# Eight places for the probability rows of attention, and smaller places for output weights and pooled copies

## The chip, the cores and the metric

The kernel runs on one core of a Trainium2 chip. The core has five engines with queues of their own: TensorE (PE in the profile) multiplies matrices out of SBUF into PSUM, VectorE (DVE) and ScalarE (ACT) do elementwise work and read PSUM, GpSimd (POOL) does elementwise work in SBUF alone, and SyncE (SP) issues most of the transfers. Each engine takes its instructions strictly in the order in which the program lists them for it; where an instruction needs what another engine makes, or a place that another engine still reads, it waits, and everything behind it in that queue waits too. The metric is the time of one execution in device microseconds, as the median of several executions.

## The reference

The reference is one layer of a transformer over 1024 latent tokens and 256 context tokens, with 1024 channels, in float32. Two attention branches read the same modulated input. Branch A is windowed (blocks of 128 queries against their neighbours within 128 positions, and the context), branch B is global (every query against all 1280 keys). Each has 8 heads of 64 channels in 2 groups, and rotary positions. Their outputs are multiplied by output weights, gated, added, projected, normalised, and sent through a gated feed-forward network with a short convolution. What this case touches is the middle of it:

```python
def _global_attention(q, k_all, v_all):
    ...
        p = jax.nn.softmax(_gqa_scores(q_blk, k_all), axis=-1)
        return _gqa_values(p, v_all)
...
def _merge_branches(o_a, o_b, gate_logits, w_branch_a, w_branch_b, w_out):
    g_a, g_b = jnp.split(jax.nn.sigmoid(gate_logits), 2, axis=-1)
    return (g_a * (o_a @ w_branch_a) + g_b * (o_b @ w_branch_b)) @ w_out
...
    h = x * (1.0 + scale1) + shift1
    y = _latent_token_mixer(h, kv_ctx, w_in[l], b_in[l], attn_sink[l], q_norm_g[l], k_norm_g[l],
                            w_branch_a[l], w_branch_b[l], w_out[l], rope)
    x = _layer_norm(DEEPNORM_ALPHA * x + gate1 * y, ln1_g[l], ln1_b[l])
    h = x * (1.0 + scale2) + shift2
    y = _conv_ffn(h, w_up[l], conv_w[l], conv_b[l], w_down[l])
    x = _layer_norm(DEEPNORM_ALPHA * x + gate2 * y, ln2_g[l], ln2_b[l])
```

## The kernel before

**Numbers.** TensorE multiplies float32 values that are rounded to a shorter form (`R32`). So each operand is split into a high part `hi`, a rounded copy, and a low part `lo`, the value less `hi`. The helper `split` does both (lines 82 and 84 for `hi`, line 87 for `lo`), on the engines named in its call. A product of two split operands takes three matmuls (`mm3`, lines 90 to 92): high by high, high by low, low by high.

**Stages.** The projections come first (to about 330 us of the span), then attention (to about 766 us), then the rest of the output weights, the output projection, the feed-forward network and the last normalisation.

**Attention units.** The work of attention is cut into 32 units of 128 queries and one group of four heads: units 0 to 15 for branch A, 16 to 31 for branch B. In its loop the program lists, at step u, the score steps of unit u and the value steps of unit u-1, and mixes them by a fraction of the step that each one is given.

- The score steps of a global unit: `cxp(0)` multiplies the queries of heads 0 and 1 by the context keys (256 columns each) into a PSUM tile `sx`, and DVE writes the scaled result into the last 256 columns of the heads' rows `p` and takes a maximum (line 555). `lat(0)` and `lat(1)` multiply by the 1024 latent keys (lines 494 and 495) into a PSUM tile `s` of two banks, DVE writes the first 1024 columns of `p` (line 542), and ACT takes the exponential of the whole row of 1280 and its sum (line 544). `cxp(2)`, `lat(2)` and `lat(3)` do the same for heads 2 and 3. `p` rows come from `p_tile`, with six places of 128 x 1280 float32. A windowed unit takes two such places, each for a pair of heads.
- The value steps of a unit: for each block n of 128 keys (ten in a global unit, four or five in a windowed one) TensorE transposes that block of all four heads' rows into one PSUM bank `ptr` (line 607). ACT casts it to `pth` (line 616), DVE subtracts to `ptl` (line 617). For one block of a windowed unit and two of a global one (`POOL_LO`), ACT copies the bank to `prw` instead (line 613), and POOL splits it. The value matmuls (lines 628 and 629) of a block come three blocks later, or five for the blocks split on POOL in a global unit, and add up in the PSUM tile `av`. After the last, `out_step` copies `av` to `avs` (ACT, line 634), adds its halves, scales them by the row sums, and splits the result into the tiles `O` (POOL mostly). `prw` and `avs` share the tag "ptr" with two places of 2 KB for each partition.

**PSUM.** Its eight banks are three `pt` tiles (for `ptr`, `sx`, the transposed queries, the sums, and the products below), two `s` tiles of two banks, and `av`.

**Output weights.** `branch_steps` multiplies `O` by the output weights of a branch. The loads `ld` fetch eight 128 x 128 blocks, which are two block columns f of the output (512 KB), into one place `wraw`, and POOL splits them into two places of the tag "whl", one for the high half and one for the low. `grp(f, hf)` then does one block column f for half hf of the tokens: 12 matmuls, and a multiplication by the stored gate on DVE (line 944). For branch A these steps are spread over the units 18 to 24 (first half of the tokens) and 25 to 30 (second half), where they stand between the attention steps. For branch B the first two block columns are listed for the end: the load in unit 31, and the four products after the loop. There `first[1]` is column 0 for the first half of the tokens, and the loop over (3, 2, 4) lists column 1 first half, column 0 second half, column 1 second half. Then follow the other block columns, from line 1078 on.

**Places.** `ht` hands out nineteen named places of 4 KB for each partition (`H0` to `H18`), first in first out; `hput` gives them back. During attention they hold the query projections (`Q`, eight), keys (`KL`, four, and `KC`), values (`VT`, five), and later the gated products `bT`.

**Order.** In the attention loop the order on each engine isn't written by hand. The framework's planner lists each engine's instructions by the program's order and by when, by its own cost model, their inputs and places are ready. In the four products after the loop the order on DVE and ACT is that of the program, and TensorE's is the planner's. From the output projection on, TensorE's order is that of the program.

Of the kernel before, what the change touches and what calls it, by code (L numbers as in the profile page):

```python
# [7 lines left out]
F32 = mybir.dt.float32  # L8
R32 = mybir.dt.float32r
# [4 lines left out]
P = 128  # L14
# [6 lines left out]
NK = T + NC  # L21
# [48 lines left out]
def layer_kernel(  # L70
# [6 lines left out]
    nc = tc.nc  # L77
    PSUM = bass.MemoryType.PSUM

    def split(src, hi, lo, hi_eng, lo_eng):  # L80
        if hi_eng is nc.scalar:
            nc.scalar.copy(hi, src)  # L82
        elif hi_eng is nc.gpsimd:
            nc.gpsimd.tensor_scalar(out=hi, in0=src, scalar1=1.0, scalar2=0.0, op0=ALU.mult, op1=ALU.add)
        else:
            hi_eng.tensor_copy(hi, src)
        lo_eng.tensor_tensor(out=lo, in0=src, in1=hi.bitcast(F32), op=ALU.subtract)  # L87

    def mm3(ps, a, b, start, stop, resumed=False):
        nc.tensor.matmul(ps, a[0], b[0], start=start, stop=False, skip_group_check=resumed)  # L90
        nc.tensor.matmul(ps, a[0], b[1], start=False, stop=False, skip_group_check=resumed)  # L91
        nc.tensor.matmul(ps, a[1], b[0], start=False, stop=stop, skip_group_check=resumed)  # L92
# [39 lines left out]
    def ht(name, shape=(P, T), dt=F32):  # L132
        hslot[name] = pool, tag = hfree.pop(0)
        return pool.tile(list(shape), dt, tag=tag, name=name, bufs=1)

    def hput(*names):
        for n in names:
            hfree.append(hslot.pop(n))
# [146 lines left out]
    for k in range(KT):  # L285
# [9 lines left out]
        h, w = hT[k], w0[k]  # L295
# [120 lines left out]
    KL, KC, VT = [], [], []  # L416
# [47 lines left out]
    class Unit:  # L464
# [133 lines left out]
        def value_steps(self):  # L598
            nm, kt = self.id, self.kt
            vh = self.br * 2 + self.g  # L600
            last = self.id == f"1_{NT - 1}_1"
            parts = {}

            def tr_step(n):
                tr = pt_tile(f"ptr{nm}_{n}")
                for h in range(4):
                    nc.tensor.transpose(tr[:, h * P:(h + 1) * P], self.pslice(h, n), ident)  # L607
                hi = att.tile([P, 512], R32, tag="pth", name=f"pth{nm}_{n}", bufs=4)
                lo = att.tile([P, 512], R32, tag="ptl", name=f"ptl{nm}_{n}", bufs=4)
                pooled = n in POOL_LO[self.br] and not last  # L610
                if pooled:
                    rw = att.tile([P, 512], F32, tag="ptr", name=f"prw{nm}_{n}", bufs=2)
                    nc.scalar.copy(rw, tr)  # L613
                    split(rw, hi, lo, nc.gpsimd, nc.gpsimd)
                else:
                    nc.scalar.copy(hi, tr)  # L616
                    nc.vector.tensor_tensor(out=lo, in0=tr, in1=hi.bitcast(F32), op=ALU.subtract)  # L617
                parts[n] = hi, lo
                return pooled

            def av_step(n):
                first = self.left == len(kt)
                self.left -= 1
                if first:
                    self.av = ps2.tile([P, 512], F32, tag="av", name=f"av{nm}")
                hi, lo = parts.pop(n)
                v = VT[kt[n] // 2][:, kt[n] % 2, vh]
                nc.tensor.matmul(self.av, v, hi, start=first, stop=False)  # L628
                nc.tensor.matmul(self.av, v, lo, start=False, stop=self.left == 0)  # L629

            def out_step():
                av = self.av
                avs = att.tile([P, 512], F32, tag="ptr", name=f"avs{nm}", bufs=2)
                nc.scalar.copy(avs, av)  # L634
                up = att.tile([HD, 512], F32, tag="up", name=f"up{nm}", bufs=1)
                nc.gpsimd.tensor_scalar(out=up, in0=avs[HD:P], scalar1=1.0, scalar2=0.0, op0=ALU.mult, op1=ALU.add)
                ot = att.tile([P, 2, P], F32, tag="ot", name=f"ot{nm}", bufs=1)
                oe = nc.gpsimd if self.br and not last else nc.vector
                for h in range(2):
                    oe.tensor_tensor(out=ot[h * HD:(h + 1) * HD],  # L640
                                     in0=avs[0:HD].rearrange("p (a b q) -> p a b q", b=2, q=P)[:, :, h],
                                     in1=up.rearrange("p (a b q) -> p a b q", b=2, q=P)[:, :, h], op=ALU.add)
                nc.gpsimd.tensor_tensor(out=ot, in0=ot, in1=self.rb, op=ALU.mult)
                hf = self.i // 4
                qs = slice((self.i % 4) * P, (self.i % 4 + 1) * P)
                split(ot, otile(self.br, hf, 0, self.g)[:, :, qs], otile(self.br, hf, 1, self.g)[:, :, qs],
                      nc.gpsimd, nc.gpsimd)

            def step(ns):
                pooled = [tr_step(n) for n in ns]  # L650
                for n, pl in zip(ns, pooled):
                    clk[0] += 1
                    avq.append((self, n, clk[0] + LAG[self.br] + (PLAG[self.br] if pl else 0)))
                    av_issue()

            self.left = len(kt)
            self.av_step, self.out_step = av_step, out_step
            g = 1 + self.br
            steps = [lambda n=n: step(range(n, n + g)) for n in range(0, len(kt), g)]
            steps.insert(3 if self.br else 2 if self.i else len(steps), self.rows)  # L660
            return steps
# [127 lines left out]
    turn = [0]  # L789
# [27 lines left out]
    for n, (gi, k) in enumerate(order):  # L817
# [19 lines left out]
        nm, src, tiles = groups[gi]  # L837
# [3 lines left out]
        w, c = ready.pop((gi, k))  # L841
        for t in tiles:
            if t < NT:
                s = slice(t * P, (t + 1) * P)
                a = hT[k][0][:, s], hT[k][1][:, s]
            else:
                s = slice((t - NT) * P, (t - NT + 1) * P)
                a = c[0][:, s], c[1][:, s]
# [36 lines left out]
    att = tc.alloc_tile_pool(name="att", bufs=1, side="right", reuse_waits="tile")  # L885
    ps2 = tc.alloc_tile_pool(name="ps2", bufs=1, space=PSUM, reuse_waits="tile")

    def pt_tile(name, dt=F32):
        return ps2.tile([P, 512], dt, tag="pt", name=name, bufs=3)
# [5 lines left out]
        return s_tile(name)[:, 0:HALF]  # L895

    def p_tile(name):
        return att.tile([P, NK], F32, tag="p", name=name, bufs=6)

    def small(name, shape):  # L900
        return att.tile(list(shape), F32, tag=name.split("_")[0], name=name,
# [19 lines left out]
    def branch_steps(br, wsrc, halves, wpool, engs, f2s=range(4)):  # L921
        steps = []
        w = {}

        def ld(f2, key):
            r = wpool.tile([P, 8, P], F32, tag="wraw", name=f"rwb{br}_{key}", bufs=1)
            nc.sync.dma_start(r, wsrc[f2])
            h = wpool.tile([P, 8, P], R32, tag="whl", name=f"hwb{br}_{key}", bufs=2)
            l = wpool.tile([P, 8, P], R32, tag="whl", name=f"lwb{br}_{key}", bufs=2)
            split(r, h, l, *engs)  # L930
            w[f2] = h, l

        def grp(f, hf, mk):
            if (br, f) not in bT:
                bT[br, f] = ht(f"bT{br}_{f}")
            b = bT[br, f][:, hf * HALF:(hf + 1) * HALF]
            nc.sync.dma_start(b, sgd[br * KT + f][:, hf * HALF:(hf + 1) * HALF])
            wh, wl = w[f // 2]
            ps = mk(f"b{br}_{f}_{hf}")
            for j in range(4):  # L940
                k = (f % 2) * 4 + j
                a = O[br, hf, 0, j // 2][:, j % 2], O[br, hf, 1, j // 2][:, j % 2]
                mm3(ps, (wh[:, k], wl[:, k]), a, j == 0, j == 3)
            nc.vector.tensor_tensor(out=b, in0=ps, in1=b, op=ALU.mult)

        for f2 in f2s:
            steps.append(lambda f2=f2: ld(f2, f"{f2}_{halves[0]}"))
            for f in (2 * f2, 2 * f2 + 1):
                for hf in halves:
                    mk = s_half if br and f % 2 and hf else pt_tile  # L950
                    steps.append(lambda f=f, hf=hf, mk=mk: grp(f, hf, mk))
        return steps

    def done(br, i, g):
# [8 lines left out]
    for u in range(nu + 1):  # L963
        vs, fs = [], []
# [10 lines left out]
        for hf, (u0, u1) in enumerate(FILL):  # L975
# [3 lines left out]
            if u0 <= u < u1:  # L979
                fs = [fill.pop(0) for e in ends if u - u0 <= e < u - u0 + 1]  # L980
# [13 lines left out]
    av_issue(True)  # L994
    nc.sync.dma_start(cvw, conv)
    nc.sync.dma_start(cvb, convb)
    hput("KC", *[f"VT{t}" for t in range(5)])

    def weight(src, nm, n=8, tag="w", he=None, le=None, rtag="raw"):
        if rtag:  # L1000
# [33 lines left out]
    def big(name):  # L1034
        return ps3.tile([P, T], F32, tag="big", name=name, bufs=3)
# [44 lines left out]
    for f in range(2, KT):  # L1080
        bT[1, f] = ht(f"bT1_{f}")
        nc.sync.dma_start(bT[1, f], sgd[KT + f])
        w = wb[f // 2]
        halves = [(0, 1)] if f < KT - 1 else [(0,), (1,)]
        for hs in halves:
            n = HALF * len(hs)
            b = bT[1, f][:, hs[0] * HALF:hs[0] * HALF + n]
            ps = big(f"b1_{f}") if len(hs) == 2 else sml(f"b1_{f}_{hs[0]}")
            for j in range(4):
                k = (f % 2) * 4 + j  # L1090
                for m, hf in enumerate(hs):
                    a = O[1, hf, 0, j // 2][:, j % 2], O[1, hf, 1, j // 2][:, j % 2]
# [233 lines left out]
    for f in (4, 6):  # L1326
        for si in (1, 2):
# [3 lines left out]
            elif f == 6:  # L1331
                (_, st), (_, dg), (_, ca), *ap = ln1(si)
                n = len(pend) - 4
# [42 lines left out]
    wsrc, wtile, wraw = {}, {}, {}  # L1376
# [333 lines left out]
    w = s.stop - s.start  # L1710
# [45 lines left out]
    r = LN2_S[1]  # L1756
# [12 lines left out]
    r = LN2_S[2]  # L1769
# [148 lines left out]
```

## Time and profile before

| What | us |
|---|---|
| Median of 3 executions | 1575.2 |
| Fastest and slowest of them | 1572.35 and 1575.25 |
| The profiled execution | 1573.05 |
| Its span, first to last instruction | 1570.9 |
| First transposition of a windowed unit | 336 |
| First transposition of a global unit | 470 |
| Last value matmul of attention | 766 |

The mean granted TensorE clock of the profiled execution was 0.996 of full speed. In the profile a name such as "p L542" is the tile that an instruction writes and its line in the kernel. A record of a matmul lasts until its modelled end, which lies after the start of the next one, so that records overlap; the time that a matmul takes from the next one is the distance between their starts. An arrow ("<-") in a timeline names what ended an engine's idle time.

### The profile page before, as it was taken

How to read it: one execution, taken by the hardware profiler on the slowest of the kernel's cores; microseconds unless marked ns; L12 is line 12 of the kernel's file. 1: busy time of each engine (PE TensorE's matmuls, PEld its weight loads, DVE VectorE, ACT ScalarE, POOL GpSimd, SP SyncE). 2: the span in 40 equal slices, each digit the busy share in tenths (PEclk: the TensorE clock that was granted, in tenths of full speed). 3: DMA queues.
4: the chain of work that ended last, by engine and by line, in shares of the span. 5: the costliest groups of instructions: out<-in, count | busy, mean ns of one | idle time of the engine just before them, and what ended most of it. 6: DMA issues, size and time to landing. Idle time of an engine off the chain costs nothing.

```text
span 1570.9 us, 22111 instructions
## 1 busy us (share of the span) xinstructions
PE 1535.7 (98%) x7804; PEld 1278.4 (81%) x7804; DVE 1181.4 (75%) x1794; ACT 787.8 (50%) x1287; POOL 754.3 (48%) x699
## 2 busy tenths in 40 slices
PE   9999999999999999999999999999999999999997
PEld 7888888888887777777788998888888888888887
DVE  6677976548887677767774789888888887657884
ACT  5322223358886566666431574544444444435552
POOL 0356423526665666655333445766677774121121
PEclk9999999999999999999999999999999999999998
DMA  9777662322246665630451223233334446996721
GB/s 370 265 239 239 213 244 86 114 76 63 64 134 145 141 163 126 139 79 27 156 187 42 81 84 116 86 118 108 111 115 111 113 113 188 366 268 211 257 98 54
DMA packets 113103, 232.09 MB, mean 148 GB/s; under 512 B 13056, under 2 KB 27904, under 8 KB 112896
## 3 DMA queue, kind: packets, MB, share of 16 engines
q1 hardware_dynamic: 97760, 201.82, 38.1%
q0 software_dynamic: 10400, 20.19, 8.3%
q10 hardware_dynamic: 4832, 8.68, 1.5%
q8 instruction: 61, 1.00, 0.3%
q14 instruction: 50, 0.41, 0.1%
HBM read 179.45 MB, written 65.86 MB: 156 GB/s over the span
## 4 chain that ended last, share of the span: by engine, by line
PE 88%; DVE 7%; ACT 2%; issue 1%; POOL 1%; DMA 0%; SPq 0%; DVEq 0%; ACTq 0%; POOLq 0%
PE ptr L607 6%; PE p L90 4%; PE p L92 4%; PE p L91 4%; PE g L90 4%; PE g L91 4%; PE g L92 4%; PE b L92 3%; PE b L90 3%; DVE p L542 3%; PE b L91 3%; PE av L628 3%; PE av L629 3%; PE s L494 2%; PE c L90 2%; PE c L91 2%
## 5 line engine op out<-in xcount | busy, mean ns | idle before, releaser
L617 DVE TENSOR_TENSOR ptl<-ptr,pth 128x512 fp32r<-128x512 f32 x190 | 124.7, 684 | 40.1 <-ACT pth L616 38.3
L607 PE MATMUL ptr<-ident,p 128*128 128x128 f32 x944 | 144.6, 278 | 8.8 <-ACT prw L613 6.0
L544 ACT ACTIVATE p<-p,nm 128x1280 f32<-128x1280 f32 (+2 forms) x128 | 139.0, 1088 | 20.5 <-DVE p L542 20.4
L607 PEld LDWEIGHTS ptr<-ident,p 128*128 128x128 f32 x944 | 109.4, 141 | 41.7 <-ACT prw L613 10.9
L87 DVE TENSOR_TENSOR ld<-rd,hd 128x1024 fp32r<-128x1024 f32 x77 | 95.0, 1250 | 49.0 <-ACT hd L82 45.3
L616 ACT CAST pth<-ptr 128x512 fp32r<-128x512 f32 x190 | 105.5, 589 | 49.5 <-PE ptr L607 39.8
L82 ACT CAST hd<-rd 128x1024 fp32r<-128x1024 f32 x77 | 79.5, 1050 | 80.4 <-PE p L92 59.0
L87 POOL TENSOR_TENSOR wlg<-wg,whg 128x512 fp32r<-128x512 f32 x32 | 46.8, 1472 | 123.5 <-ACT whg L82 84.5
L90 PE MATMUL p<-hd 128*128 128x512 f32 x264 | 103.2, 391 | 0.0
L92 PE MATMUL p<-hd,ld 128*128 128x512 f32 x264 | 102.8, 389 | 0.0
L91 PE MATMUL p<-ld,hd 128*128 128x512 f32 x264 | 102.7, 389 | 0.0
L628 PE MATMUL av<-pth,VT 128*128 128x512 f32 x236 | 101.4, 430 | 0.7 <-ACT avs L634 0.4
L90 PE MATMUL g<-hh,whg 128*128 128x512 f32 x256 | 99.9, 390 | 0.0
L629 PE MATMUL av<-ptl,VT 128*128 128x512 f32 x236 | 99.4, 421 | 0.4 <-POOL ptl L87 0.4
L92 PE MATMUL g<-hh,wlg 128*128 128x512 f32 x256 | 99.7, 389 | 0.0
L91 PE MATMUL g<-hl,whg 128*128 128x512 f32 x256 | 99.6, 389 | 0.0
L494 PE MATMUL s<-KL,q 128*128 128x512 f32 (+2 forms) x192 | 79.5, 414 | 9.1 <-DVE p L542 7.9
L542 DVE TENSOR_SCALAR_CACHE_REDUCE p<-s,cvt,nmc 128x1024 f32<-128x1024 f32 x64 | 84.5, 1340 | 0.0
L495 PE MATMUL s<-KL,q 128*128 128x512 f32 (+2 forms) x192 | 73.0, 380 | 0.0
L780 ACT ACTIVATE sg<-g,bgc 128x512 f32<-128x512 f32 x32 | 22.0, 686 | 96.2 <-PE g L92 91.5
L82 ACT CAST wS<-s 128x512 fp32r<-128x512 f32 x76 | 45.3, 620 | 46.4 <-POOL s L1220 45.7
L82 ACT CAST wA<-ru 128x512 fp32r<-128x512 f32 x57 | 35.5, 623 | 64.1 <-PE d L92 35.2
(427 smaller groups left out, 4897.6 us busy)
## 6 DMA issues: line engine op xcount, KB each, us to landing
wml<-in_wmodT_dram SPq DMA_DIRECT2D x48, 512.0 KB
ru<-in_w_up_dram SPq DMA_DIRECT2D x38, 512.0 KB
rd<-td SPq DMA_DIRECT2D x55, 256.0 KB
rd<-sd SPq DMA_DIRECT2D x44, 256.0 KB
rd<-in_w_dn_dram SPq DMA_DIRECT2D x33, 256.0 KB
wm<-in_wmodT_dram SPq DMA_DIRECT2D x16, 512.0 KB
wg<-in_w_g_dram SPq DMA_DIRECT2D x32, 256.0 KB
sgd<-sg ACTq DMA_DIRECT2D x32, 256.0 KB
```

Of the source, the lines that this page charges most:

```text
L82: nc.scalar.copy(hi, src)
L87: lo_eng.tensor_tensor(out=lo, in0=src, in1=hi.bitcast(F32), op=ALU.subtract)
L90: nc.tensor.matmul(ps, a[0], b[0], start=start, stop=False, skip_group_check=resumed)
L91: nc.tensor.matmul(ps, a[0], b[1], start=False, stop=False, skip_group_check=resumed)
L92: nc.tensor.matmul(ps, a[1], b[0], start=False, stop=stop, skip_group_check=resumed)
L494: nc.tensor.matmul(o, self.q[0][:, hs], ks, start=True, stop=False)
L542: nc.vector.tensor_scalar(out=out, in0=o, scalar1=self.qscale(nqs)[:, hs] if self.br else -1.0, scalar2=self.other[:, hs], op0=ALU.mult, o ...
L544: nc.scalar.activation(row, row, AF.Exp, bias=self.nm[:, hs], scale=-1.0, accum_out=self.sm[:, hs])
L607: nc.tensor.transpose(tr[:, h * P:(h + 1) * P], self.pslice(h, n), ident)
L617: nc.vector.tensor_tensor(out=lo, in0=tr, in1=hi.bitcast(F32), op=ALU.subtract)
L628: nc.tensor.matmul(self.av, v, hi, start=first, stop=False)
L629: nc.tensor.matmul(self.av, v, lo, start=False, stop=self.left == 0)
```

## The change

The rows `p` get eight places instead of six. The copies `prw` and `avs` leave the tag "ptr" and take, in turn, one half each of a place of `ht` named "side", which is given back after the loop with those of the context keys and values. The output weights are loaded by one block column (256 KB): the raw data have one place ("wraw"), the high parts two ("whl"), the low parts one of their own ("wlo"). The first two columns are loaded in one step, and each further one after the products of the column two before it. The number of matmuls and the elements that are split and copied stay as they were.

```diff
-                    rw = att.tile([P, 512], F32, tag="ptr", name=f"prw{nm}_{n}", bufs=2)
+                    rw = side_tile()
...
-                avs = att.tile([P, 512], F32, tag="ptr", name=f"avs{nm}", bufs=2)
+                avs = side_tile()
...
     def p_tile(name):
-        return att.tile([P, NK], F32, tag="p", name=name, bufs=6)
+        return att.tile([P, NK], F32, tag="p", name=name, bufs=8)
+
+    side = ht("side", (P, 2, 512))
+    turn = [0]
+
+    def side_tile():
+        turn[0] ^= 1
+        return side[:, turn[0]]
...
-        def ld(f2, key):
-            r = wpool.tile([P, 8, P], F32, tag="wraw", name=f"rwb{br}_{key}", bufs=1)
-            nc.sync.dma_start(r, wsrc[f2])
-            h = wpool.tile([P, 8, P], R32, tag="whl", name=f"hwb{br}_{key}", bufs=2)
-            l = wpool.tile([P, 8, P], R32, tag="whl", name=f"lwb{br}_{key}", bufs=2)
+        def ld(f, key):
+            l = wpool.tile([P, 4, P], R32, tag="wlo", name=f"lwb{br}_{key}", bufs=1)
+            r = wpool.tile([P, 4, P], F32, tag="wraw", name=f"rwb{br}_{key}", bufs=1)
+            nc.sync.dma_start(r, wsrc[f // 2][:, (f % 2) * 4:(f % 2) * 4 + 4])
+            h = wpool.tile([P, 4, P], R32, tag="whl", name=f"hwb{br}_{key}", bufs=2)
             split(r, h, l, *engs)
-            w[f2] = h, l
+            w[f] = h, l
...
-        for f2 in f2s:
-            steps.append(lambda f2=f2: ld(f2, f"{f2}_{halves[0]}"))
-            for f in (2 * f2, 2 * f2 + 1):
-                for hf in halves:
-                    mk = s_half if br and f % 2 and hf else pt_tile
-                    steps.append(lambda f=f, hf=hf, mk=mk: grp(f, hf, mk))
+        fs = [f for f2 in f2s for f in (2 * f2, 2 * f2 + 1)]
+        steps.append(lambda: [ld(f, f"{f}_{halves[0]}") for f in fs[:2]])
+        for n, f in enumerate(fs):
+            for hf in halves:
+                mk = s_half if br and f % 2 and hf else pt_tile
+                steps.append(lambda f=f, hf=hf, mk=mk: grp(f, hf, mk))
+            if n + 2 < len(fs):
+                steps.append(lambda f=fs[n + 2]: ld(f, f"{f}_{halves[0]}"))
...
-    hput("KC", *[f"VT{t}" for t in range(5)])
+    hput("KC", "side", *[f"VT{t}" for t in range(5)])
```

More of the change, by code (lines that the diff above doesn't have):

```diff
@@ L937, in grp @@
             nc.sync.dma_start(b, sgd[br * KT + f][:, hf * HALF:(hf + 1) * HALF])
-            wh, wl = w[f // 2]
+            wh, wl = w[f]
             ps = mk(f"b{br}_{f}_{hf}")
             for j in range(4):
-                k = (f % 2) * 4 + j
                 a = O[br, hf, 0, j // 2][:, j % 2], O[br, hf, 1, j // 2][:, j % 2]
-                mm3(ps, (wh[:, k], wl[:, k]), a, j == 0, j == 3)
+                mm3(ps, (wh[:, j], wl[:, j]), a, j == 0, j == 3)
             nc.vector.tensor_tensor(out=b, in0=ps, in1=b, op=ALU.mult)
-        for f2 in f2s:
-            steps.append(lambda f2=f2: ld(f2, f"{f2}_{halves[0]}"))
-            for f in (2 * f2, 2 * f2 + 1):
-                for hf in halves:
-                    mk = s_half if br and f % 2 and hf else pt_tile
-                    steps.append(lambda f=f, hf=hf, mk=mk: grp(f, hf, mk))
+        fs = [f for f2 in f2s for f in (2 * f2, 2 * f2 + 1)]
[6 more added lines that the diff above has]
+                steps.append(lambda f=fs[n + 2]: ld(f, f"{f}_{halves[0]}"))
         return steps
```

## The prediction

> **What bounds the kernel now.** I read the page first, parts 1 and 2, for what is busy.
>
> ```profile
> span 1570.9 us, 22111 instructions
> PE 1535.7 (98%) x7804; PEld 1278.4 (81%) x7804; DVE 1181.4 (75%) x1794; ACT 787.8 (50%) x1287; POOL 754.3 (48%) x699
> ```
>
> TensorE is busy for 98% and nothing else comes near, so at first sight only 35 us (1570.9 less 1535.7) are to be had. But a matmul record overlaps the next one, so short gaps hide in it. The busy time by stages gives the true price of a matmul, and shows where the kernel falls short of it: a stretch of the up projection, twelve units of global attention (units 17 to 28, from the first transposition of one to that of another), and seven units of windowed attention (5 to 11).
>
> ```profile
> 1000.00:1300.00 300.00, 300.00 (x1325) 248.40 (x1325) 263.63 (x231) 144.66 (x205) 208.07 (x118) 1.00 0.38 113
> ...
> 489.03:719.20 230.17, 219.01 (x1238) 173.77 (x1236) 162.79 (x315) 145.40 (x242) 140.50 (x166) 1.00 0.52 123
> ...
> 386.16:443.59 57.43, 57.43 (x386) 49.57 (x386) 50.06 (x120) 51.09 (x120) 38.06 (x56) 1.00 0.25 68
> ```
>
> In the first, all matmuls are 512 wide and follow without a gap: 300/1325 = 0.2264 us each. The groups of TensorE's lines in the second stretch, shapes kept apart, are what has to be priced:
>
> ```profile
> L607 PE MATMUL ptr<-ident,p 128*128 128x128 f32 x481 | 68.8, 275 | 5.1 <-ACT prw L613 5.1
> L628 PE MATMUL av<-pth,VT 128*128 128x512 f32 x120 | 51.1, 426 | 0.0
> L629 PE MATMUL av<-ptl,VT 128*128 128x512 f32 x120 | 49.9, 416 | 0.0
> L494 PE MATMUL s<-KL,q 128*128 128x512 f32 x97 | 42.8, 441 | 6.1 <-DVE p L542 5.2
> L495 PE MATMUL s<-KL,q 128*128 128x512 f32 x96 | 38.9, 405 | 0.0
> L92 PE MATMUL b<-O,lwb 128*128 128x512 f32 x56 | 22.0, 392 | 0.0
> L90 PE MATMUL b<-O,hwb 128*128 128x512 f32 x56 | 21.9, 392 | 0.0
> L91 PE MATMUL b<-O,hwb 128*128 128x512 f32 x56 | 21.9, 390 | 0.0
> L495 PE MATMUL sx<-KC,q 128*128 128x256 f32 x48 | 12.4, 280 | 0.0
> L494 PE MATMUL sx<-KC,q 128*128 128x256 f32 x48 | 12.4, 280 | 0.0
> ```
>
> The price of a transposition comes from the timeline, late in unit 31:
>
> ```profile
> 763.24 1.03 PE L607 MATMUL ptr<-ident,p 128*128 128x128 f32 x8
> 764.03 0.48 PE L628 MATMUL av<-pth,VT 128*128 128x512 f32 x1
> 764.35 0.39 PE L629 MATMUL av<-ptl,VT 128*128 128x512 f32 x1
> ```
>
> Eight of them and one value matmul take 764.35 - 763.24 = 1.11 us; less 0.2264 that is 0.11 each. A 256 wide matmul is 0.115 (next fence: 544.83 to 544.94 is 0.11). So the twelve units hold 601 x 0.2264 + 481 x 0.11 + 96 x 0.115 = 136.1 + 52.9 + 11.0 = 200 us, and about 3 us for the small transpositions of queries and sums (48 and 12 of them, at half a transposition as an estimate). Of 230.2 us, **27 us are gaps: 2.25 us in each unit of 19.2**. There are sixteen such units. The vector engines are no bound there: DVE 162.8/230.2 = 71%, ACT 63%, POOL 61%.
>
> What makes the gap, from the chain that ended last, then TensorE's timeline at the same place (the change from unit 19 to 20):
>
> ```profile
> 542.95 0.56 PE ptr L607 x5
> ...
> 543.53 0.90 DVE p L555 x4
> 544.43 2.54 DVE p L542 x4
> ```
>
> ```profile
> 544.83 0.28 PE L494 MATMUL sx<-KC,q 128*128 128x256 f32 x1
> 544.94 0.28 PE L495 MATMUL sx<-KC,q 128*128 128x256 f32 x1
> 545.75 0.50 PE L494 MATMUL s<-KL,q 128*128 128x512 f32 x1 [0.53 <-DVE p L542]
> ...
> 546.55 0.39 PE L495 MATMUL s<-KL,q 128*128 128x512 f32 x1
> 547.02 0.50 PE L494 MATMUL s<-KL,q 128*128 128x512 f32 x1
> ...
> 549.78 0.48 PE L495 MATMUL s<-KL,q 128*128 128x512 f32 x1
> 550.70 0.66 PE L607 MATMUL ptr<-ident,p 128*128 128x128 f32 x4 [0.44 <-ACT prw L613]
> ```
>
> The last transpositions of unit 19 end; at once DVE writes the context columns of heads 2 and 3 (line 555), and behind them the latent columns (line 542) that TensorE's two score banks wait for. Starts less prices give three gaps: 545.75 - 544.94 - 0.115 = 0.69, 547.02 - 546.55 - 0.226 = 0.24, 550.70 - 549.78 - 0.226 = 0.69, and two late seconds of 0.11: 1.85 us, most of the 2.25. It is so at every change of unit:
>
> ```profile
> DVE p L555 <- PE ptr L607: 12.6, 15, 0.9
> ...
> PE ptr L607 <- ACT prw L613: 6.0, 14, 0.4
> PE s L494 <- DVE p L542: 5.9, 14, 0.5
> ```
>
> Fifteen times DVE sat idle at line 555 until transpositions were done. The reason is in the code: a global unit takes four `p` rows, all four are read by every transposed group, so unit u-1 holds four until its last group, and of six places unit u gets two. Heads 2 and 3 must wait, then two 1.34 us evictions, two exps, and ACT's casts queue behind those exps: a burst.
>
> **The change part by part.** *Eight p places.* Nothing is computed more or less. Units u-1 and u fit together, so line 555 for heads 2 and 3 waits for unit u-2's rows, long free; evictions and exps spread over the unit as the program's order has them. What of the 2.25 us goes? At most the 1.85 us counted. At least, I judge by windowed attention: there a unit takes two pair rows of the six, nothing waits for `p`, and with DVE and ACT at 87% and 89% TensorE shows no idle time at all (57.43 of 57.43), where the twelve global units show 230.17 - 219.01 = 11.16, 0.93 a unit. So 0.93 to 1.85, over 15 changes of unit 14 to 28 us; I take 1.4, the middle, since part of the hidden gaps will stay behind ACT's exps and the three `pt` banks: **-21 us**. If nothing at all moves, 0 (a rival below). Nor is a loss excluded, since the planner orders every engine's queue anew.
>
> The last unit pays more now, and the granted clock (last but two column) falls after its wait:
>
> ```profile
> 754.45 0.99 PE L607 MATMUL ptr<-ident,p 128*128 128x128 f32 x4 [1.81 <-ACT p L544]
> ...
> 754.00:756.00 2.00, 1.41 (x7) 1.01 (x8) 1.36 (x4) 1.74 (x4) 0.00 (x0) 0.89 0.14 43
> 756.00:758.00 2.00, 1.88 (x9) 1.37 (x8) 0.83 (x2) 1.45 (x4) 0.00 (x0) 0.50 0.03 8
> 758.00:760.00 2.00, 2.00 (x12) 1.87 (x13) 1.37 (x3) 1.19 (x3) 1.15 (x2) 0.76 0.00 0
> ```
>
> 1.98 us of gap (1.81 and a hidden 0.17), then 2 x (0.11 + 0.50 + 0.24) = 1.7 us of clock. With its rows written early both go: **-3.7 us** (0 to 3.7).
>
> *Output weights by halves.* Each load of eight blocks becomes two of four: bytes, products and elements split are equal; sixteen more DMA issues and POOL instructions lie beside TensorE work, at nothing. What is new: `l` (tag "wlo") has one place. The low half of block column f+1 is written only when all products of f are done. In the filled units the products of one column stand most of a unit apart, so the 1.3 us write hides behind other matmuls. POOL queues pair splits and output steps behind that wait, SP the next raw half; bound by the same kind of wait now (next rival), 0 here.
>
> At the end nothing hides it. After the last value matmul TensorE now runs product (0, first half), then (1, first half), 24 matmuls, which just cover the output step of unit 31:
>
> ```profile
> 766.21 0.39 PE L629 MATMUL av<-ptl,VT 128*128 128x512 f32 x1
> ...
> 770.33 1.58 POOL L87 TENSOR_TENSOR O<-ot,O 128x256 fp32r<-128x256 f32 x1
> ...
> L87 POOL TENSOR_TENSOR ptl<-prw,pth 128x512 fp32r<-128x512 f32 x24 | 30.9, 1289 | 2.0
> ...
> L87 POOL TENSOR_TENSOR lwb<-rwb,hwb 128x1024 fp32r<-128x1024 f32 x7 | 17.4, 2491 | 0.3
> ```
>
> 24 x 0.2264 from 766.44 ends at 771.87; `O` is done at 771.91. After the change `l` of column 1 waits for both products of column 0, and the second of these waits for `O`. So (1, first half) stops at its third matmul: 766.44 + 14 x 0.2264 = 769.61, a gap of 2.3 us to `O`; then 12 matmuls, then POOL's subtraction (1.29 by the first row, 2491/2 = 1.25 by the second) with its signals 1.4 us. And 2.3 us is more than the 1.98 after which the clock fell, so by that row 1.7 us more. Sum **+5.4 us**, bounds 2.3 (later products fill the second gap, clock stays) and 5.4.
>
> [...]
>
> *The side place.* `prw` and `avs` keep two places of 2 KB in turn, now halves of one projection place. During attention 8 Q, 4 KL, 1 KC and 5 VT places of 19 are taken, so one is free; the same ACT copies go there: 0. Later tiles shift by one place; the cast of the second output weights (hwb1, ACT) moves from a Q place to one that unit 30's scores read, so 1.05 us of ACT comes late, used only after the four last products: 0.
>
> Sum: -21 - 3.7 + 5.4 = **-19.3 us**. The profiled execution took 1573.05 us as a run, 2.15 under the median of 1575.2, with runs from 1572.35; so 1553.7 to 1555.9, and I say 1555.
>
> **The rivals.** *The burst moves only in part.* The wait for ACT's copy (0.69 a unit) stays because ACT must still pass the exps, and one score gap stays: 0.6 x 15 = 9 us go, with the last unit's 3.7, against 5.4: -7.3, 1567. For it: ACT's casts and copies share one queue with 1.37 us exps, and three `pt` banks serve ten groups a unit. Against it: windowed attention does that at a higher load without visible idle time.
>
> *It doesn't do what it says.* The planner keeps heads 2 and 3 behind the transpositions, or the score banks hold them back as before: no gain, the tail's +5.4: 1580. Against it: DVE's wait at line 555 names the transpositions 15 times of 15.
>
> *POOL stands still (slower).* The low half's subtraction waits in POOL's queue for TensorE's product of the column before; behind it stand pair splits that value matmuls need. Today's wait of that kind:
>
> ```profile
> POOL hwb L84 <- PE b L91: 5.5, 4, 1.7
> ```
>
> Four times in the attention stages, at most 1.7 us. If each of the 14 later loads of both passes costs TensorE 1.7 us, that is +23.8, in all +4.5: 1578 to 1580. It decides from 19.3/14 = 1.4 us a load. Against it: value matmuls of pooled pairs are issued five groups after their transposition, a longer time than that wait.
>
> **How the numbers follow.** Forecast 0.62, in part 0.18, no effect 0.08, POOL 0.07, and 0.05 for something that leaves it within 0.2%, about 3 us, which is what a measurement of this kernel can tell from no change. The forecast's own range is -28 - 3.7 + 2.3 = -29.4 to -14 + 5.4 = -8.6, so 1544 to 1566; to hold 8 in 10 it reaches through the partial case to 1569. Faster: 0.62 + 0.18 = 0.80 less a little, 0.79; same 0.06; slower 0.15.
>
> **What would show it.** Right: DVE no longer idle at line 555 until transpositions; exps of a unit spread over it; twelve units in less than 215 us; no 1.81 us wait in the last unit; after the last value matmul about 14 matmuls, then a wait for `O`, and one for the low half on POOL, perhaps with a lower clock. Wrong: the gaps before line 494 as long as now; waits of value matmuls (lines 628, 629) for POOL; or the tail without a gap, if the planner found other work.

## The result, and the profile after

The changed kernel takes 1551.5 us against 1574.1 us for the kernel before, both medians of four executions: a ratio of 0.9857 with a 95% interval of 0.984 to 0.9874, or 22.6 us less. The prediction had 1555 us, from a sum of -19.3 us. The profiled execution after took 1550.34 us. This is its page:

```profile
span 1548.6 us, 22178 instructions
## 1 busy us (share of the span) xinstructions
PE 1526.3 (99%) x7804; PEld 1279.8 (83%) x7804; DVE 1182.9 (76%) x1794; ACT 788.2 (51%) x1287; POOL 754.6 (49%) x717
```

TensorE has the same 7804 matmuls; only 9.4 us less of busy time is shown, because much of what went was hidden in overlapping records. The busy times by stages have the same twelve units (17 to 28), now from 485.92 to 698.30:

```profile
485.92:698.30 212.38, 210.98 (x1235) 174.56 (x1234) 163.65 (x316) 144.97 (x242) 143.07 (x180) 1.00 0.57 137
```

They last 212.4 us instead of 230.2, or 17.7 a unit instead of 19.2, and 1.40 us of visible idle time is left of 11.16. DVE, ACT and POOL work as long as before (163.7, 145.0 and 143.1 us against 162.8, 145.4 and 140.5), only closer together.

Why the gaps went can be read from the waits between 470 and 752 us, DVE's first, then TensorE's (engine and line, who was waited for, us in total, times, longest):

```profile
DVE p L555 <- PE sx L495: 6.5, 7, 1.0
...
PE av L629 <- POOL ptl L87: 1.1, 2, 0.7
PE b L92 <- POOL lwb L87: 0.9, 1, 0.9
...
PE b L91 <- POOL O L87: 0.6, 1, 0.6
```

Line 555 doesn't wait for transpositions any more, where it did 15 times; what it waits for is its own input `sx`. The two waits of TensorE that stood on top before (line 494 for DVE, `ptr` for ACT's copy, 5.9 and 6.0 us) are gone from the list or down to single ones. The change from unit 19 to 20, shown before with its burst, now looks like this on DVE and then on TensorE, in order of time:

```profile
529.47 0.48 DVE L555 TENSOR_SCALAR_CACHE_REDUCE p<-sx,cvt 128x256 f32<-128x256 f32 x1
...
530.27 1.34 DVE L542 TENSOR_SCALAR_CACHE_REDUCE p<-s,cvt,nmc 128x1024 f32<-128x1024 f32 x1
...
532.40 1.23 DVE L542 TENSOR_SCALAR_CACHE_REDUCE p<-s,cvt,nmc 128x1024 f32<-128x1024 f32 x1
```

```profile
534.29 0.60 PE L607 MATMUL ptr<-ident,p 128*128 128x128 f32 x4
...
536.39 0.62 PE L607 MATMUL ptr<-ident,p 128*128 128x128 f32 x4
```

Heads 2 and 3 of unit 20 are written from 529.5 on, five microseconds before the last transposed group of unit 19 (534.29), and the first group of unit 20 follows 2.1 us later without a wait.

**Where the time went.** I priced every matmul as the prediction does (0.2264 us for 512 columns, 0.11 for a float32 transposition, and for fewer columns in proportion, which is an estimate: 0.113 for 256, where two starts lie 0.11 us apart in the kernel before, 544.83 and 544.94, and 0.12 in the changed one, 534.84 and 534.96) and took the prices from the length of each stage. What is left are the gaps, in us:

| Profiled execution of | windowed units | global units | 16 us after the last transposition |
|---|---|---|---|
| before | 17.9 | 36.4 | 0.1 |
| changed | 16.5 | 13.4 | 2.2 |
| changed, second and third | 16.5, 16.5 | 15.8, 15.3 | 2.2, 2.2 |

Global units gave 23.0 us (20.6 and 21.1 in the other two), windowed ones 1.4, and the tail took 2.0 back: 22.4 us, and the span fell by 22.3.

The tail is what the prediction had looked for, but smaller. Here are TensorE, then POOL, then the busy times by 2 us, with the granted clock as the last but two column:

```profile
746.38 0.39 PE L90 MATMUL b<-O,hwb 128*128 128x512 f32 x1
747.32 0.50 PE L91 MATMUL b<-O,hwb 128*128 128x512 f32 x1 [0.55 <-POOL O L87]
...
748.81 0.40 PE L91 MATMUL b<-O,hwb 128*128 128x512 f32 x1
750.15 0.50 PE L92 MATMUL b<-O,lwb 128*128 128x512 f32 x1 [0.94 <-POOL lwb L87]
```

```profile
745.69 1.57 POOL L87 TENSOR_TENSOR O<-ot,O 128x256 fp32r<-128x256 f32 x1
748.82 1.27 POOL L87 TENSOR_TENSOR lwb<-rwb,hwb 128x512 fp32r<-128x512 f32 x1 [1.56 <-PE b L92]
```

```profile
746.00:748.00 2.00, 1.45 (x7) 0.90 (x6) 0.68 (x1) 0.01 (x1) 1.26 (x1) 1.00 0.90 363
748.00:750.00 2.00, 1.21 (x6) 0.64 (x4) 0.00 (x0) 0.00 (x0) 1.18 (x1) 1.00 1.04 426
750.00:752.00 2.00, 1.85 (x8) 1.55 (x9) 0.00 (x0) 0.00 (x0) 0.09 (x1) 1.00 0.65 264
```

There are two gaps: 747.32 - 746.38 - 0.23 = 0.71 us until `O` is split, and 750.15 - 748.81 - 0.23 = 1.11 us until POOL has written the low half of column 1, which it may do only after the last product with column 0's. Behind each, the second matmul starts 0.33 us after the first (747.65 after 747.32, 750.48 after 750.15), 0.1 us more than the price. The clock stays at 1.00.

### The profile page after: what moved, and what is told of

It reads as the page before. It is cut to its first block, busy times and chain, and to the rows that moved or that the text cites. A ratio compares the mean times of both kernels' runs of the same rounds, so it can differ in the third digit from the quotient of the medians.

```text
span 1548.6 us, 22178 instructions
## 1 busy us (share of the span) xinstructions
PE 1526.3 (99%) x7804; PEld 1279.8 (83%) x7804; DVE 1182.9 (76%) x1794; ACT 788.2 (51%) x1287; POOL 754.6 (49%) x717
## 4 chain that ended last, share of the span: by engine, by line
PE 48%; DVE 2%; issue 1%; ACT 0%; POOL 0%; DVEq 0%; ACTq 0%
PE p L92 4%; PE p L90 4%; PE p L91 4%; PE c L90 2%; PE d L90 2%; PE c L91 2%; PE d L91 2%; PE c L92 2%; PE d L92 2%; PE a L90 2%; PE a L91 2%; PE a L92 2%; PE b L92 2%; PE b L90 2%; PE b L91 2%; PE y L90 2%
## 5 line engine op out<-in xcount | busy, mean ns | idle before, releaser
L544 ACT ACTIVATE p<-p,nm 128x1280 f32<-128x1280 f32 (+2 forms) x128 | 139.1, 1088 | 16.1 <-DVE p L542 15.8
L494 PE MATMUL s<-KL,q 128*128 128x512 f32 (+2 forms) x192 | 75.2, 392 | 1.1 <-DVE p L542 0.9
L495 PE MATMUL s<-KL,q 128*128 128x512 f32 (+2 forms) x192 | 72.3, 377 | 0.0
```

The lines of the kernel that those rows point to most:

```text
L544: nc.scalar.activation(row, row, AF.Exp, bias=self.nm[:, hs], scale=-1.0, accum_out=self.sm[:, hs])
```

## The experiments

### Is it the number of places?

The changed kernel ran again, and also with six and seven places for `p`. With six, everything else stays as changed.

```diff
-        return att.tile([P, NK], F32, tag="p", name=name, bufs=8)
+        return att.tile([P, NK], F32, tag="p", name=name, bufs=6)
```

> The changed kernel once more, for comparison on the same chip: 22 to 23 us below the kernel before, ratio 0.986. Both theories expect the same.

> The changed kernel with six p places instead of eight; the halves of weights, the side place and the tail stay as changed. Theory A (the gain is the two more places): the wait of DVE at line 555 for the last transpositions comes back 15 times, the gaps of about 2.1 us in each global unit too, and the tail's 2.0 us stays, so 1 to 3 us slower than the kernel before (ratio 1.001 to 1.002). Theory B (finer loads of weights on POOL, or the planner's new order, gave a part of the gain): clearly faster than the kernel before, by 5 us or more.

> The changed kernel with seven p places. Theory A: head 2 of a unit finds a place early and only head 3 waits for the last transpositions, so the burst behind them is one eviction and one exp instead of two; about half of the gain is there: 8 to 14 us below the kernel before. Theory B (a whole pair of heads has to fit): as with six places, within 3 us of the kernel before.

| Kernel | Median us | Ratio to before | 95% interval | gaps: windowed, global, tail |
|---|---|---|---|---|
| changed, again | 1552.8 | 0.9864 | 0.9851 to 0.9878 | 16.5, 15.8, 2.2 |
| seven places | 1559.0 | 0.9904 | 0.989 to 0.9917 | 16.4, 21.7, 2.2 |
| six places | 1574.4 | 1.0001 | 0.9992 to 1.001 | 16.5, 37.0, 2.2 |

With six places the whole gain is gone. In the waits of DVE the old line is back, with the same count; this is the row of the six places, and below it that of the seven:

```profile
DVE p L555 <- PE ptr L607: 11.0, 15, 0.9
...
DVE p L555 <- PE ptr L607: 16.8, 15, 2.4
```

So the finer loads, the side place and the planner's new order, taken alone, give none of it in global units: their gaps are 37.0 us with them and 36.4 without. They do account for the 1.4 us in windowed units, which is there with six places as well; by unit, 0.9 of it lies in unit 0 and 0.5 in unit 15. By the gaps six places are 0.6 - 1.4 + 2.1 = 1.3 us longer than the kernel before, as theory A expected. The medians lie 0.2 us apart, with an interval of -1.3 to 1.6, so they can't tell 1.3 us from none. Which of the parts gives the 1.4 us wasn't tried.

With seven places 15.3 us of 21.4 are gained, more than the half that was expected. The wait at line 555 is still there 15 times and even longer, probably since DVE reaches it earlier, but only one row stands behind it.

### The tail

The low half of column 1 gets a place of its own: a `p` place, which is free as soon as unit 30's rows are transposed. The load, `first[5]`, is listed after the loop.

```diff
-            l = wpool.tile([P, 4, P], R32, tag="wlo", name=f"lwb{br}_{key}", bufs=1)
+            if br and f == 1:
+                l = wpool.tile([P, 4, P], R32, tag="p", name=f"lwb{br}_{key}", bufs=8)
+            else:
+                l = wpool.tile([P, 4, P], R32, tag="wlo", name=f"lwb{br}_{key}", bufs=1)
...
     av_issue(True)
+    first[5]()
```

> The changed kernel, but the low half of the second column of the last output weights gets a p place of its own, loaded after the loop. Theory: product (1, first half) can again run while the output step of unit 31 is under way; both gaps of the tail (0.8 us for O, 1.2 us for the low half) go, and with them 2.0 us: 1.5 to 2.5 us below the changed kernel. Rival: the time moves into a later wait (the evictions after the loop, or the second weights), and nothing is gained.

> The changed kernel, beside the next one on the same chip: 1551 to 1553 us.

> The low half of the second column in a p place, a second time, since its gaps were gone in the trace (2.18 us in the 16 us after the last transposition to 0.14) while the times, three against four, lay 1.3 us apart with intervals that overlap. Theory: 2 us under the changed kernel, 1549 to 1551. Rival: the same time as the changed kernel.

In both traces the gaps of the 16 us after the last transposition fell from 2.18 to 0.14 us, the value of the kernel before. The first time the executions were 1549.3, 1550.7 and 1552.4 us (a fourth of 5424 us is left out), and ratios 0.9852 (0.9837 to 0.9867) and 0.9864 (0.9851 to 0.9878) overlap. The second time it was 1550.4 against 1552.7 us, 0.9852 (0.9838 to 0.9867) against 0.9868 (0.9853 to 0.9882). Taken together, seven executions have a mean of 1550.5 us and the twelve of the changed kernel 1552.3: 1.8 us, with a standard error of 0.6 from their spread. This version is faster than both kernels: 0.9852.

### When does the clock fall?

The prediction charged the tail 1.7 us for the clock, since it fell in unit 31 after a gap of 1.98 us. To have gaps of other lengths at one place, POOL writes the low half of column 1 once or twice more. By the prediction the clock falls behind both gaps; the other possibility is that the shorter one leaves it at 1.00 and costs its own length alone.

```diff
             split(r, h, l, *engs)
+            for _ in range(1 if br and f else 0):
+                nc.gpsimd.tensor_tensor(out=l, in0=r, in1=h.bitcast(F32), op=ALU.subtract)
```

> The changed kernel; POOL computes the low half of the second column of the last output weights twice, so the gap of TensorE before it grows from 1.2 to 2.5 us. Theory of the prediction (a gap of 2 us is enough for the clock to fall, as in unit 31 before): the granted clock falls to 0.5 behind the gap and the stage pays 1.3 us for the gap and some 1.7 us for the clock. [...]

> The same with the low half computed three times, a gap of 3.8 us. Both theories expect the clock to fall: 2.6 us for the gap and about 1.7 us for the clock.

TensorE's matmul behind the gap and the busy times of the stages around it, for one more:

```profile
752.58 0.50 PE L92 MATMUL b<-O,lwb 128*128 128x512 f32 x1 [2.28 <-POOL lwb L939]
...
752.00:754.00 2.00, 1.42 (x6) 1.18 (x7) 0.00 (x0) 0.00 (x0) 0.52 (x1) 1.00 0.37 150
754.00:756.00 2.00, 2.00 (x11) 1.63 (x10) 0.79 (x2) 0.00 (x0) 0.00 (x0) 1.00 0.00 0
```

and for two more:

```profile
753.91 0.80 PE L92 MATMUL b<-O,lwb 128*128 128x512 f32 x1 [3.63 <-POOL lwb L939]
...
752.00:754.00 2.00, 0.09 (x1) 0.09 (x1) 0.00 (x0) 0.00 (x0) 1.78 (x2) 0.74 0.24 96
754.00:756.00 2.00, 2.00 (x5) 1.63 (x6) 0.00 (x0) 0.00 (x0) 0.00 (x0) 0.50 0.00 0
756.00:758.00 2.00, 2.00 (x6) 1.54 (x6) 0.00 (x0) 0.00 (x0) 0.00 (x0) 0.50 0.00 0
758.00:760.00 2.00, 2.00 (x7) 1.59 (x6) 1.38 (x3) 0.00 (x0) 0.00 (x0) 0.55 0.00 0
```

A gap of 2.45 us (752.58 less 749.90, where the matmul ahead of it starts, less 0.23) cost its own length and nothing else: the clock stays at 1.00, and the tail's gaps grow from 2.18 to 3.54 us. A gap of 3.79 us (753.91 - 749.89 - 0.23) was followed by nearly 6 us at half clock, the 0.50 and 0.55 of the rows above. Gaps in the 40 us after the last transposition grow from 2.2 to 7.6 us; 2.7 of these are the longer gap and 2.8 the clock. So the prediction's reading failed for the shorter gap, with one execution of each. The length of the gap alone doesn't order the three: 1.98 us in the kernel before lowered the clock to 0.50, and 2.45 us here left it at 1.00. What else decides was not shown.

### What is left of the gaps

Units 19 to 23 are down to 0.41 to 0.50 us, but unit 24 has 1.7 and unit 28 1.5. Unit 16, the first global one, has 2.0, and in the second profile unit 18 has 2.2; their cause stays open. At the end of unit 24 a value matmul waits for POOL. These are POOL and TensorE there, in the changed kernel:

```profile
620.96 0.62 POOL L84 TENSOR_SCALAR hwb<-rwb 128x512 fp32r<-128x512 f32 x1 [2.67 <-DMA rwb<-in_w_a_dram]
621.54 0.62 POOL L84 TENSOR_SCALAR pth<-side 128x512 fp32r<-128x512 f32 x1
...
622.50 1.28 POOL L87 TENSOR_TENSOR ptl<-side,pth 128x512 fp32r<-128x512 f32 x1
...
623.83 0.50 PE L629 MATMUL av<-ptl,VT 128*128 128x512 f32 x1 [0.66 <-POOL ptl L87]
```

POOL stood 2.67 us at the cast of a raw half that hadn't landed, with a pair split behind it. But it also waits at the sums of down weights (line 678). Two kernels tell these apart. The first leaves the accumulating transfers out, and with them the sums. The second fetches the raw half of branch A's weights once, so that later columns use the weights of the first.

```diff
-            for m in more:
-                nc.gpsimd.dma_start(t, m, accum_op=ALU.add)
```

> The changed kernel without the accumulating transfers that POOL issues for the sums of down weights in global units (line 678); the sums are left out of the computation. Theory (what is left of the gaps in units 18 and 24 to 28 comes from POOL, which stands in its queue until an earlier transfer has landed, with a pair split behind it): those units fall to about 0.45 us of gap like units 19 to 23, 4 to 6 us in all. Rival (it is the raw halves of weights that land late, or the two places of the pair copies): the gaps stay within 1 us in sum.

```diff
-            r = wpool.tile([P, 4, P], F32, tag="wraw", name=f"rwb{br}_{key}", bufs=1)
-            nc.sync.dma_start(r, wsrc[f // 2][:, (f % 2) * 4:(f % 2) * 4 + 4])
+            if br or not kept:
+                r = wpool.tile([P, 4, P], F32, tag="wraw", name=f"rwb{br}_{key}", bufs=1)
+                nc.sync.dma_start(r, wsrc[f // 2][:, (f % 2) * 4:(f % 2) * 4 + 4])
+                kept.append(r)
+            r = r if br else kept[0]
```

> The changed kernel, but the raw half of branch A's output weights is fetched once and split again for every column, so later columns use the first one's weights. Theory (what is left in units 24 and 28 is POOL standing at the cast of a raw half that hasn't landed, with a pair split behind it): POOL no longer waits for raw halves, units 24 and 28 fall from 1.5 to 2 us of gap to below 0.8, the sixteen global units together by 2 to 4 us, and the time by as much. Rival (three pt banks, or the value order): units 24 and 28 stay above 1.3.

POOL's longest wait in the changed kernel, and then in the one without sums:

```profile
POOL hwb L84 <- DMA rwb<-in_w_a_dram: 19.9, 10, 2.8
```

```profile
POOL hwb L84 <- DMA rwb<-in_w_a_dram: 34.2, 14, 3.0
```

Without the sums the time is 1553.2 us (0.9866, 0.9852 to 0.9879), units 24 and 28 keep 2.0 and 1.7 us, and the global units 14.9 us. The theory of the sums fell: POOL only waits longer at the next thing, the raw half (34.2 us, where three profiles of the changed kernel have 19.9, 27.3 and 25.2). With one raw half that row is gone, the time is 1548.1 us (0.9841, 0.9824 to 0.9857), 4.5 us under the changed kernel on the same chip, and the global units have 11.7 us of gaps; unit 28 has 0.8 us and unit 24 1.1, a little more than expected. So waiting for raw halves costs the changed kernel about 4 us, and that is the next thing to mend. A second raw place wasn't tried.

Before that was known, the sums were moved, together with the low half in a `p` place:

```diff
-DNS = {u0 + 2 * n + (u0 == 20): (n, j0, j1) for u0, j0, j1 in ((16, 0, 4), (20, 4, 8), (24, 8, 11)) for n in range(3)}
+DNS = {u0 + 2 * n + (u0 == 8): (n, j0, j1) for u0, j0, j1 in ((4, 0, 4), (8, 4, 8), (12, 8, 11)) for n in range(3)}
```

> The kernel with the low half in a p place, and the sums of down weights listed in units 4 to 16 instead of 16 to 28, where half as much is transferred. If POOL's standing in global units costs 4 to 6 us, and windowed units have room for it: 3 to 6 us below the kernel with the low half in a p place, some 26 us below the kernel before. If windowed units, where DVE and ACT are nearly full, pay the same: no gain.

It took 1571.5 us (0.9984, 0.9975 to 0.9993), 20 us more than without the move. Windowed units went from 16.5 to 37.0 us of gaps, global ones stayed at 16.3. Here are units 6 to 13 of it, and windowed units 6 to 12 of the changed kernel:

```profile
386.55:470.95 84.40, 72.97 (x443) 61.82 (x443) 61.03 (x137) 58.83 (x138) 54.41 (x72) 0.92 0.98 236
```

```profile
385.00:442.49 57.49, 57.49 (x387) 49.63 (x386) 50.11 (x120) 51.14 (x120) 38.09 (x56) 1.00 0.25 68
```

The DMA engines are busy for 98% there and TensorE stands idle for 11 us. The clock is at 0.92 on average, which is up to 6.8 us of the loss (an estimate, 0.08 x 84.40). Its waits, from 336 to 489 us, name DVE, and the copies of the queries that go through a transfer; POOL stands at the sums:

```profile
PE s L494 <- DVE p L542: 7.0, 5, 2.5
...
PE s L495 <- DMA q<-q: 3.3, 3, 1.4
```

```profile
POOL sd L678 <- DMA sd<-in_w_dn_dram: 10.0, 3, 4.2
POOL sd L678 <- DMA sd<-sd: 9.6, 3, 4.4
```

Which of these two, the late query copies or POOL's standing, weighs more in windowed units stays open.

## Why the prediction was right, and where it wasn't

- **What bounds the kernel: right.** The four `p` rows of a unit, read by every transposed group, held heads 2 and 3 of the next unit back. Six, seven and eight places give 0, 15 and 21 us. (The windowed units that the prediction calls 5 to 11 are 6 to 12, counted from 0.)
- **Eight places, -21 us: right.** Units 16 to 30 went from 32.0 to 12.1 us of gaps, by 19.9 in the first profile and by about 18 in the other two, or 1.2 to 1.3 a unit where 1.4 was taken between 0.93 and 1.85. That the visible idle time would go entirely, as in windowed units, was nearly so: 1.40 us in twelve units.
- **The last unit, -3.7 us: right.** Its gaps went from 4.4 to 1.3 us, by 3.1, and with the 1.81 us wait the low clock behind it went: it is 1.00 in the changed kernel from 7.02 to 1539.60 us. With six places the wait is back, at 2.03 us.
- **The tail, +5.4 us: the mechanism right, the size wrong; +2.0.** Two of three terms were too dear. The gap until `O` was 0.8 us and not 2.3, since product (0, second half) reads two tiles of `O` that unit 30 had finished; seven matmuls of it ran first. The clock did not fall (1.00 in the three stages from 746 to 752 us), 0 and not 1.7. The low half's term was 1.2 us where 1.4 was taken. The measured 2.0 lies just under this part's lower bound of 2.3.
- **The clock.** The step that failed is "by that row 1.7 us more": one gap's length was taken for what lowers the clock. The tail had no gap of 2.3 us to begin with; its two were 0.71 and 1.11 us, 1.82 in all, and the clock stayed at 1.00. And where a gap of 2.45 us was put, longer than the 1.98 us after which the clock had fallen, it stayed at 1.00 too; after 3.79 us it was at 0.50. These runs don't show by what the fall after 1.98 us came.
- **Loads by halves hidden in the filled units, 0 us: wrong by about 4, once the units are packed.** Not the wait for the product of the column before, which the prediction named, but the landing of the raw half stops POOL, 10 times for 19.9 us in all. The wait is new: in the kernel before, POOL never waits for a raw block during attention. With six places it is there too, 9 times for 22.9 us, and global units have only 0.6 us more gaps than before, so its price depends on what else holds TensorE back. The rival "POOL stands still" thus holds in that POOL stands, but at another wait, and at 4.5/14 = 0.3 us a load and not the 1.4 from which it would have decided.
- **The side place and the shifted places, 0 us.** In windowed units 1.4 us went that no term had.

So the sum of -19.3 fell 3.3 us short of -22.6. The tail, priced 3.4 us too high, and the 1.4 us of windowed units made it too small; the two large terms, 1.1 and 0.6 us too large by the first profile, hid a part of that. In the two repetitions the gain is 21.1 to 21.4 us.

## What to carry to other kernels

Count how many places a producer needs from what its reader still holds, not from what is made at a time: where every read touches all rows of a unit, places for one and a half units serialise two units, and one place short of two units still gives most. A busy share of 98% said nothing here of 36 us of gaps in one stage; starts less prices did. When room is made by single places elsewhere, look for the queue that stands at them, and for the end of the stage, where nothing else is left to run.

## What the runs showed of the hardware

Three gaps of TensorE and what followed: 1.98 us (the kernel before, unit 31), then mainly transpositions, clock down to 0.50; 2.45 us (one more write of the low half), then matmuls, clock at 1.00; 3.79 us (two more), then matmuls, nearly 6 us at half clock, 2.8 us lost by the prices, an estimate. The shortest but not the middle one lowered the clock, so in these three executions the length of the gap is not what orders them.

Sixteen matmuls of a single column each take 2.14 us (857.67 to 859.81 in the kernel before, 835.12 to 837.26 in the changed one), most of them 0.11 us from one start to the next. Prices in proportion to the columns, an estimate, make them hardly any work.
